# Latent attention's matmuls put in one chain in source order, with the score tiles taken two key tiles at a time

## The chip, the cores and the metric

The kernel runs on one core of a Trainium2 chip. The metric is the device time of one launch in microseconds, as the median of several runs. The engines that matter are TensorE (PE for its matmuls, PEld for its weight loads), VectorE (DVE), ScalarE (ACT) and GpSimd (POOL). Each engine takes its instructions from a queue of its own and in the order of that queue.

## The reference, cut to what matters

The reference is a two-layer network over 1024 latent tokens and 256 context tokens (T = 1280 columns in the kernel, context first), width 1024. Each layer projects its input, mixes tokens in three head groups (gated linear attention, retention, and eight heads of multi-head latent attention), projects out, and runs a gated convolutional feed-forward part. The change touches only the latent attention, which is:

```
s = (einsum('bqhd,bkhd->bhqk', qn, kn) + einsum('bqhr,bkr->bhqk', qr, kr)) * MLA_SCALE
p = softmax(s)
out = einsum('bhqk,bkhe->bqhe', p, v)
```

A latent query sees all 1280 keys. A context query sees the 256 context keys, and is needed in layer 0 alone. Everything is float32.

## The kernel before, in words

The program is one core's instruction stream, traced by a tile framework. The framework knows what each instruction reads and writes. At compile time its scheduler walks through all of them, with its own estimate of their durations, and fixes the order of every engine's queue: of the instructions whose inputs it takes to be ready, the earlier in the source goes first, but one that is not ready is passed by a later one. On the chip the order of each queue is then fixed, and semaphores hold an instruction until what it depends on is done. A manual dependency of the class NoSync adds an edge for the scheduler alone. It adds no semaphore between two instructions of one engine.

In each layer `tile_hybrid_kernel` (L1247) runs the projections, then `weave` (L1233) interleaves two generators: `lin` (L817; linear attention and retention) takes 1.5 steps for each step of `mla` (L826). Their instructions share PE, DVE, ACT and POOL. After them come the output projection and the feed-forward part, whose matmuls are on L323 and L1188.

`mla` handles the heads one after the other. For a head and one tile of 128 keys (`kt`), queries come in two blocks of 512 (`i`). `products` (L938, matmul on L942) makes one score tile of 128 keys by 512 queries with three matmuls that add up in one PSUM bank (high part times high part, and two cross terms with a low part; operands of type float32r). ACT takes the exponential on L1026 into the buffer `held[kt]`, which has room for both query blocks. `values` (L944, matmul on L948) multiplies the exponentials with the values. It issues two plain float32 matmuls, one for each query block, each with 64 columns of weights and 512 moving columns, and they write the lower and upper 64 partitions of bank 6. A float32 matmul is executed as two instructions, so one call of `values` appears as four PE instructions (x4) in the trace.

The source order before: for each key tile, query block 0's three score matmuls, a piece of side work, query block 1's three, a piece of side work, then `values` of the key tile two earlier. The sum of the exponentials is kept by additions on POOL (L1037, key tiles 1 to 6) and DVE (L1035, key tiles 8 and 9; L1043 joins both). The buffers come from a ring of seven (`w2`, L123).

The side work (`beside`, two generator steps after each score tile) prepares the next head: `prod_kq` (L885) makes its keys and queries by matmuls on L903 and L906, which take PSUM banks 0 to 2 at once, with copies by ACT (L912) and DVE (L913). `maxima` (L916) then finds each query's largest score: 24 matmuls (26 in layer 0) on L925, each into one of the banks 0 to 2 in turn, and each followed by a maximum on DVE (L926) that frees the bank. L928, L932 and two DMAs through DRAM bring the negative maxima into row 96 of the next head's queries, which is the 97th row of its score matmuls. Every second head `prod_v` (L854, L858) makes the values of two heads; `prod_qr` (L864) runs twice per layer. `quotient` (L951) ends a head: it copies bank 6, sums the exponentials over keys by matmuls with ones (L959) into one of the banks 0 to 2, takes the reciprocal on DVE (L960) and multiplies on DVE (L963); `tail` runs one step of it. The score tiles rotate through banks 3 to 5.

Of `lin`, the lines that appear below are L739 and L727 (matmuls), L643 and L647 (matmuls of a chunk's output).

Of the kernel before, what the change touches and what calls it, by code (L numbers as in the profile page):

```python
# [9 lines left out]
F32 = mybir.dt.float32  # L10
# [10 lines left out]
CTX = 256  # L21
# [53 lines left out]
class Net:  # L75
# [750 lines left out]
    def mla(self, l, S):  # L826
# [24 lines left out]
        def three():  # L851
            return self.ps[:, base[0]:base[0] + 3, :].rearrange("p a b -> p (a b)")

        def prod_v(p):  # L854
            V[p] = [self.hid([128, 5, 128]) for _ in range(2)]
            ps = three()
            for t_ in range(10):
                nc.tensor.matmul(ps[:, 128 * t_:128 * t_ + 128], S.ckv[:, 128 * t_:128 * t_ + 128], wk[:, 1, 128 * p:128 * p + 128],  # L858
                                 start=True, stop=True)
            for i in range(2):  # L860
                nc.scalar.copy(V[p][i][:].rearrange("p a b -> p (a b)"), ps[:, 640 * i:640 * i + 640])
            yield

        def prod_qr(x):  # L864
            QR[x] = [self.yk(F32R), self.yk(F32R)]
            ps, raw = three(), QR[x][1]
            chunks = [(o, min(512, T - o), ps[:, o - lo:min(512 + o, T) - lo]) for o in range(lo, T, 512)]
            for o, n, t in chunks:
                for kc in range(2):
                    nc.tensor.matmul(t, wr[:, kc, 128 * x:128 * x + 128], S.cq[kc][:, o:o + n], start=(kc == 0), stop=(kc == 1))  # L870
                nc.scalar.copy(raw[:, o:o + n].bitcast(F32), t)
            for o, n, t in chunks:
                r = raw[:, o:o + n].bitcast(F32)
                t2, co, si = self.tt([128, 512]), self.tt([128, 512]), self.tt([128, 512])
                nc.sync.dma_start(co[:, 0:n], a["mcos"][:, o:o + n])
                nc.sync.dma_start(si[:, 0:n], a["msin"][:, o:o + n])
                nc.tensor.matmul(t, self.permm[:], r, start=True, stop=True)
                nc.vector.tensor_tensor(t2[:, 0:n], t, si[:, 0:n], op=ALU.mult)
                nc.vector.tensor_tensor(r, r, co[:, 0:n], op=ALU.mult)
                nc.vector.tensor_tensor(r, r, t2[:, 0:n], op=ALU.add)  # L880
                self.split(QR[x][0][:, o:o + n], raw[:, o:o + n], r)
                del t2, co, si
            yield

        def prod_kq(h):  # L885
            K = Kt[h % 2]
            Q[h] = [self.hs([128, T]) for _ in range(2)]
            rr = slice(32 * (h % 4), 32 * (h % 4) + 32)
            for x in range(2):
                for o in range(lo, T, 512):  # L890
                    c = slice(o, min(o + 512, T))
                    nc.sync.dma_start(Q[h][x][64:96, c].bitcast(F32), QR[h // 4][x][rr, c].bitcast(F32))
            if h < 2:
                for b in range(2):
                    cs = slice(640 * b, 640 * b + 640)
                    self.split(K[0][64:96, cs], K[1][64:96, cs], S.kr[b][64:96, :])
            if h == 1:
                S.kr.clear()
            yield
            ps = three()  # L900
            for o, t, kb in ((CTX, ps[:, 0:512], 1), (CTX + 512, ps[:, 512:1024], 1), (0, ps[:, 1024:1280], 0)):
                n = 512 if kb else CTX
                nc.tensor.matmul(t[0:64, 0:n], wk[:, 0, 64 * h:64 * h + 64], S.ckv[:, o:o + n], start=True, stop=True, skip_group_check=True)  # L903
                if o >= lo:
                    for kc in range(2):
                        nc.tensor.matmul(t[64:128, 0:n], wn[:, kc, 64 * h:64 * h + 64], S.cq[kc][:, o:o + n],  # L906
                                         start=(kc == 0), stop=(kc == 1), skip_group_check=True)
            for o, t, n in ((CTX, ps[:, 0:1024], 1024), (0, ps[:, 1024:1280], CTX)):
                for X, r in ((K, 0), (Q[h], 64)):
                    if r and o < lo:  # L910
                        continue
                    nc.scalar.copy(X[0][0:64, o:o + n], t[r:r + 64])  # L912
                    nc.vector.tensor_tensor(X[1][0:64, o:o + n], t[r:r + 64], X[0][0:64, o:o + n].bitcast(F32), op=ALU.subtract)  # L913
            yield

        def maxima(h):  # L916

            k0, q0 = Kt[h % 2][0], Q[h][0]
            mx, part = self.sm([128, 10]), self.sm([128, 8, 3])
            for qi in range(lo // 128, 10):  # L920
                nk = CTX if qi < 2 else T
                for j, o in enumerate(range(0, nk, 512)):
                    n = min(512, nk - o)
                    t = bank("pre")[:, 0:n]
                    nc.tensor.matmul(t, q0[0:96, 128 * qi:128 * qi + 128], k0[0:96, o:o + n], start=True, stop=True)  # L925
                    nc.vector.tensor_reduce(mx[:, qi:qi + 1] if qi < 2 else part[:, qi - 2, j:j + 1], t, axis=AX.X, op=ALU.max)  # L926
                    yield
            nc.vector.tensor_reduce(mx[:, 2:10], part[:], axis=AX.X, op=ALU.max)  # L928
            yield
            n = 10 - lo // 128  # L930
            t, r = bank("pre"), self.dgt()
            nc.tensor.matmul(t[0:n, 0:128], mx[:, 10 - n:10], self.ident[:], start=True, stop=True)  # L932
            nc.scalar.activation(r[0:n, :], t[0:n, 0:128], AF.Copy, scale=-1.0)
            nc.sync.dma_start(S.mx[h, 10 - n:10, :], r[0:n, :].bitcast(F32))
            nc.sync.dma_start(q0[96:97, lo:T].bitcast(F32), S.mx[h:h + 1].rearrange("h a b -> h (a b)")[:, lo:T])
            yield

        def products(h, kt, c0, t):  # L938

            n = t.shape[-1]  # L940
            for x, (qa, ka, rows) in enumerate(((0, 0, 97), (1, 0, 96), (0, 1, 96))):
                nc.tensor.matmul(t, Kt[h % 2][ka][0:rows, 128 * kt:128 * kt + 128], Q[h][qa][0:rows, c0:c0 + n], start=(x == 0), stop=(x == 2))  # L942

        def values(h, kt, P, n, last):  # L944
            r = 64 * (h % 2)
            op = self.pb("av")
            for i in range(2):
                nc.tensor.matmul(op[64 * i:64 * i + 64, 0:n], V[h // 2][kt // 5][:, kt % 5, r:r + 64], P[:, i], start=(kt == 0), stop=last,  # L948
                                 skip_group_check=True)

        def quotient(h, c0, n, P):  # L951

            r = 64 * (h % 2)
            o, ov, rb = ob[h // 2], self.tt([128, n]), self.tt([128, n])
            nc.scalar.copy(ov[:], self.pb("av")[:, 0:n])
            yield
            t = bank("pre")[:, 0:n]
            for i in range(2):
                nc.tensor.matmul(t[64 * i:64 * i + 64, :], self.ones[:, 0:64], P[:, i], start=True, stop=True, skip_group_check=True)  # L959
            nc.vector.reciprocal(rb[:], t)  # L960
            yield
            for i in range(2):
                nc.vector.tensor_tensor(o[r:r + 64, c0 + n * i:c0 + n * i + n], ov[64 * i:64 * i + 64, :], rb[64 * i:64 * i + 64, :], op=ALU.mult)  # L963
            if h % 2:
                nc.sync.dma_start(S.m[:, 4 + h // 2, c0:c0 + 2 * n], o[:, c0:c0 + 2 * n])
            yield
# [3 lines left out]
                yield from g  # L970

        tails = []

        def tail():
            if tails and next(tails[0], self) is self:
                tails.pop(0)
# [7 lines left out]
        for h in range(8):  # L984
# [11 lines left out]
            def beside(n=2):  # L996
                for _ in range(n):
                    next(side, None)
# [17 lines left out]
                del P  # L1016
                yield
            held = {}
            for kt in range(12):
                if kt < 10:  # L1020
                    held[kt] = self.w2([128, 2, 512], F32)
                for i in range(2):
                    if kt < 10:
                        t = bank("sc")
                        products(h, kt, CTX + 512 * i, t)
                        nc.scalar.activation(held[kt][:, i], t, AF.Exp, scale=MSCALE)  # L1026
                        beside()
                    if i == 0:
                        tail()
                    elif kt >= 2:  # L1030
                        k = kt - 2
                        P = held[k]
                        values(h, k, P, 512, k == 9)
                        if k in (8, 9):
# [3 lines left out]
                        if k not in (0, 7):  # L1038
                            del held[k]
                        del P  # L1040
                    if kt < 10:
                        yield
            nc.vector.tensor_tensor(held[0][:], held[0][:], held[7][:], op=ALU.add)  # L1043
            tails.append(quotient(h, CTX, 512, held[0]))
            tail()
# [431 lines left out]
```

## Time and profile before

| what | value |
|---|---|
| median of 3 runs | 3635.89 us (3632.38 to 3640.07) |
| the profiled execution's own time | 3636.93 us |
| its span, first to last instruction | 3635.2 us |
| PE busy over the span | 3471.4 us (95%) |
| DVE / ACT / POOL busy | 2331.7 / 1410.1 / 561.8 us |
| mean granted clock of TensorE | 0.968 |

A busy PE is a PE with a matmul in flight, not one at its peak. Two stretches hold the woven attention: 365 to 905 us (layer 0) and 2325 to 2768 us (layer 1). In a timeline row the first number is the start, the second the time that the merged row is busy; where the next matmul starts is in the next row.

### The profile page before, as it was taken

What the parts mean: (1) busy time and instruction counts of PE and PEld (TensorE: products, weight loads), DVE (VectorE), ACT (ScalarE), POOL (GpSimd) and SP (SyncE); (2) the same over time, 40 slices, a digit from 0 to 9 for tenths busy, and PEclk for the clock granted to TensorE, in tenths of its full rate; (3) what the DMA queues carried; (4) which work ended last, traced back from release to release, by engine and by line L of the source; (5) the groups of instructions that cost most, each with busy time, mean ns of one, the idle gap of its engine ahead of it and who ended that gap; (6) DMA issues with size and microseconds to landing.
All of it is one profiled execution on the core that took longest, in us unless ns stands there. A gap on an engine that the chain in (4) does not pass through costs nothing. (4 is left out here: it accounts for less than half of the span.)

```text
span 3635.2 us, 50748 instructions
## 1 busy us (share of the span) xinstructions
PE 3471.4 (95%) x20270; PEld 2749.7 (76%) x20270; DVE 2331.7 (64%) x3371; ACT 1410.1 (39%) x2355; POOL 561.8 (15%) x583
## 2 busy tenths in 40 slices
PE   8998999997999999999999999889999999999998
PEld 6995544443999999899999897444446788888897
DVE  4336678777676445675557734878776875577555
ACT  3333333333354332343334443333333554345433
POOL 0001454444011000000000000453441000000001
PEclk9998899998999999999999999899999999999999
DMA  8653011021322333432223444011114222323221
GB/s 293 199 175 112 26 31 46 30 82 63 126 72 99 118 118 130 156 103 78 76 76 115 154 132 138 23 35 38 33 48 155 93 93 93 97 90 116 94 95 51
DMA packets 174702, 354.63 MB, mean 98 GB/s; under 512 B 15648, under 2 KB 92912, under 8 KB 174464
## 3 DMA queue, kind: packets, MB, share of 16 engines
q1 hardware_dynamic: 174464, 351.38, 29.5%
q8 instruction: 159, 2.61, 0.3%
q14 instruction: 79, 0.65, 0.1%
HBM read 310.09 MB, written 36.51 MB: 95 GB/s over the span
## 5 line engine op out<-in xcount | busy, mean ns | idle before, releaser
L323 PE MATMUL ps<-h,w 128*128 128x320 f32 (+5 forms) x9600 | 1681.6, 336 | 27.5 <-ACT h L212 16.4
L323 PEld LDWEIGHTS ps<-h,w 128*128 128x128 f32 x9600 | 1539.6, 190 | 166.3 <-ACT h L212 18.7
L213 DVE TENSOR_TENSOR w<-ws,w 128x1024 fp32r<-128x1024 f32 x360 | 440.2, 1223 | 589.7 <-PE ps L323 289.1
L1188 PE MATMUL ps<-hid,w 128*128 128x256 f32 (+4 forms) x3696 | 576.3, 316 | 1.5 <-ACT hid L212 1.5
L1188 PEld LDWEIGHTS ps<-hid,w 128*128 128x128 f32 x3696 | 538.9, 189 | 35.9 <-issue 7.6
L212 ACT CAST w<-ws 128x1024 fp32r<-128x1024 f32 x360 | 379.1, 1054 | 415.4 <-PE ps L1188 290.9
L1026 ACT ACTIVATE w<-ps 128x512 f32<-128x512 f32 x320 | 188.7, 596 | 338.5 <-PE ps L942 332.4
L942 PE MATMUL ps<-h,h 96*128 96x512 f32 (+3 forms) x1008 | 318.7, 431 | 0.3 <-ACT w L1026 0.2
L942 PEld LDWEIGHTS ps<-h,h 96*128 96x128 f32 (+1 forms) x1008 | 183.3, 199 | 151.8 <-issue 92.2
L926 DVE TENSOR_REDUCE sm<-ps 128x1 f32<-128x512 f32 (+1 forms) x400 | 221.7, 585 | 92.2 <-PE ps L925 90.3
L1037 POOL TENSOR_TENSOR w<-w,w 128x1024 f32<-128x1024 f32 x96 | 238.7, 2487 | 271.1 <-PE ps L948 173.0
L948 PE MATMUL ps<-w,hid 128*64 128x512 f32 (+1 forms) x704 | 276.0, 614 | 0.3 <-ACT w L1005 0.3
L1145 POOL MEMSET u<- 128x1 f32 (+1 forms) x264 | 21.5, 103 | 1613.4 <-DVE t L1156 1486.7
L1155 DVE SCALAR_TENSOR_TENSOR t<-u,vec,t 128x642 f32<-128x642 f32 (+3 forms) x176 | 144.6, 822 | 183.8 <-ACT t L1154 183.6
L1149 ACT COPY u<-ps 128x512 f32<-128x512 f32 (+4 forms) x264 | 118.4, 483 | 316.3 <-PE ps L323 316.3
L1193 DVE SCALAR_TENSOR_TENSOR y<-ps,mod,y 128x320 f32<-128x320 f32 (+5 forms) x376 | 197.1, 558 | 68.5 <-PE ps L1188 68.0
L925 PE MATMUL ps<-h,h 96*128 96x512 f32 (+1 forms) x400 | 156.1, 440 | 34.5 <-DVE sm L926 25.3
L925 PEld LDWEIGHTS ps<-h,h 96*128 96x128 f32 x400 | 77.8, 206 | 126.5 <-DVE sm L926 66.6
L716 POOL TENSOR_TENSOR hid<-hid,hid 128x512 f32<-128x512 f32 x108 | 153.3, 1439 | 83.0 <-ACT hid L696 56.2
L1154 ACT ACTIVATE t<-u,vec 128x642 f32<-128x642 f32 (+3 forms) x176 | 153.7, 873 | 0.4
L1156 DVE SCALAR_TENSOR_TENSOR t<-u,vec,t 128x642 f32<-128x642 f32 (+3 forms) x176 | 144.3, 820 | 11.4
L212 ACT CAST hid<-t 128x642 fp32r<-128x642 f32 (+3 forms) x88 | 59.5, 676 | 204.8 <-DVE t L1160 204.8
(197 smaller groups left out, 3134.4 us busy)
## 6 DMA issues: line engine op xcount, KB each, us to landing
ws<-in_up_dram SPq DMA_DIRECT2D x176, 512.0 KB
ws<-in_down_dram SPq DMA_DIRECT2D x88, 512.0 KB
ws<-in_ada_dram SPq DMA_DIRECT2D x80, 512.0 KB
ws<-in_w_in_dram SPq DMA_DIRECT2D x48, 512.0 KB
ws<-in_w_out_dram SPq DMA_DIRECT2D x32, 512.0 KB
y<-in_ada_dram SPq DMA_DIRECT2D x16, 512.0 KB
ws<-in_w_v_dram SPq DMA_DIRECT2D x16, 512.0 KB
hid<-in_xT_dram SPq DMA_DIRECT2D x16, 320.0 KB
```

What stands on the lines that cost most here:

```text
L212: self.nc.scalar.copy(hi, src)
L213: self.nc.vector.tensor_tensor(lo, src, hi.bitcast(F32), op=ALU.subtract)
L323: nc.tensor.matmul(ps[:, i, 0:n], w_[:, k, :], h[k][:, part, o:o + n], start=(k == 0 and q == 0), stop=(k == 7 and q == 2))
L925: nc.tensor.matmul(t, q0[0:96, 128 * qi:128 * qi + 128], k0[0:96, o:o + n], start=True, stop=True)
L926: nc.vector.tensor_reduce(mx[:, qi:qi + 1] if qi < 2 else part[:, qi - 2, j:j + 1], t, axis=AX.X, op=ALU.max)
L942: nc.tensor.matmul(t, Kt[h % 2][ka][0:rows, 128 * kt:128 * kt + 128], Q[h][qa][0:rows, c0:c0 + n], start=(x == 0), stop=(x == 2))
L948: nc.tensor.matmul(op[64 * i:64 * i + 64, 0:n], V[h // 2][kt // 5][:, kt % 5, r:r + 64], P[:, i], start=(kt == 0), stop=last, skip_group_c ...
L1026: nc.scalar.activation(held[kt][:, i], t, AF.Exp, scale=MSCALE)
L1037: nc.gpsimd.tensor_tensor(held[0][:], held[0][:], P[:], op=ALU.add)
L1154: nc.scalar.activation(v[:, 0:n], u[:, 1:1 + n], AF.Identity, scale=cw(j, 1), bias=self.vec[l][:, V_CB + j:V_CB + j + 1])
L1188: nc.tensor.matmul(pb[i][:, 0:n], w[w_][:, x, ms], p.hh[f0 + x][hp][:, o - 1:o - 1 + n], start=(x == 0 and q == 0), stop=(x == gn - 1 and ...
L1193: nc.vector.scalar_tensor_tensor(t, pb[i][:, o:o + n], self.md(l, 5, m, who), t, op0=ALU.mult, op1=ALU.add)
```

## The change

Every matmul that `mla` issues goes through a new function `pin`, which makes each depend, for the scheduler alone, on the one that `mla` issued before it. So PE's queue holds all of `mla`'s matmuls in the order of the source. `lin`'s matmuls are not pinned and may still be placed between any two of them. And the loop over key tiles takes two at a time: both tiles' four score tiles (twelve matmuls) with their side work, then a step of the tail, then `values` of the two preceding key tiles, one after the other. The number of steps that the generator yields for a head stays 20.

```diff
+        prev = [None]
+
+        def pin(x):
+
+            if prev[0] is not None:
+                self.tc.add_manual_dep(x.ins, prev[0].ins.name, mybir.DependencyInfo(mybir.DependencyClass.NoSync, mybir.DependencyReason.DATA),
+                                       reason="in order")
+            prev[0] = x
+
...
-                nc.tensor.matmul(t, Kt[h % 2][ka][0:rows, 128 * kt:128 * kt + 128], Q[h][qa][0:rows, c0:c0 + n], start=(x == 0), stop=(x == 2))
+                pin(nc.tensor.matmul(t, Kt[h % 2][ka][0:rows, 128 * kt:128 * kt + 128], Q[h][qa][0:rows, c0:c0 + n], start=(x == 0), stop=(x == 2)))
...
-            for kt in range(12):
+            for kt in range(0, 12, 2):
                 if kt < 10:
-                    held[kt] = self.w2([128, 2, 512], F32)
-                for i in range(2):
-                    if kt < 10:
-                        t = bank("sc")
-                        products(h, kt, CTX + 512 * i, t)
-                        nc.scalar.activation(held[kt][:, i], t, AF.Exp, scale=MSCALE)
-                        beside()
-                    if i == 0:
-                        tail()
-                    elif kt >= 2:
-                        k = kt - 2
+                    for k in (kt, kt + 1):
+                        held[k] = self.w2([128, 2, 512], F32)
+                        for i in range(2):
+                            t = bank("sc")
+                            products(h, k, CTX + 512 * i, t)
+                            nc.scalar.activation(held[k][:, i], t, AF.Exp, scale=MSCALE)
+                            beside()
+                            if k == kt or i == 0:
+                                yield
+                tail()
+                if kt >= 2:
+                    for k in (kt - 2, kt - 1):
                         P = held[k]
                         values(h, k, P, 512, k == 9)
...
-                    if kt < 10:
-                        yield
+                if kt < 10:
+                    yield
```

The matmuls of `prod_v`, `prod_qr`, `prod_kq`, `maxima`, `values` and `quotient` are wrapped in `pin` in the same way.

## Rows read from the trace of the kernel before

**Rows 1.** The page's first part: busy time, share, instructions.
```profile
PE 3471.4 (95%) x20270; PEld 2749.7 (76%) x20270; DVE 2331.7 (64%) x3371; ACT 1410.1 (39%) x2355; POOL 561.8 (15%) x583
```

**Rows 2.** Windows: stretch, us, then PE, PEld, DVE, ACT, POOL busy; clock, DMA.
```profile
365.00:905.00 540.00, 491.47 (x2208) 243.66 (x2208) 411.54 (x564) 188.94 (x394) 237.32 (x141) 0.91 0.15 46
2325.00:2768.00 443.00, 411.10 (x1798) 200.54 (x1796) 341.31 (x436) 157.45 (x308) 198.10 (x114) 0.95 0.16 50
...
617.00:628.00 11.00, 8.93 (x48) 5.18 (x49) 10.21 (x13) 3.23 (x9) 8.08 (x6) 0.54 0.18 50
750.00:850.00 100.00, 89.94 (x438) 43.99 (x437) 87.45 (x118) 35.61 (x81) 46.72 (x28) 0.97 0.24 78
850.00:910.00 60.00, 43.20 (x181) 20.74 (x181) 36.65 (x45) 18.07 (x29) 14.03 (x13) 0.84 0.27 86
```

**Rows 3.** Windows of line L948 alone: PE and PEld busy, clock, DMA.
```profile
365.00:905.00 540.00, 146.84 (x384) 30.49 (x384) 0.91 0.15 46
2325.00:2768.00 443.00, 123.77 (x304) 24.17 (x304) 0.95 0.16 50
```

**Rows 4.** PE's timeline in layer 0: start, busy us, line, tiles, shape, count.
```profile
503.25 1.08 PE L948 MATMUL ps<-w,hid 128*64 128x512 f32 x4
504.25 1.66 PE L942 MATMUL ps<-h,h 97*128 97x512 f32 x6
505.84 0.64 PE L948 MATMUL ps<-w,hid 128*64 128x512 f32 x1
...
511.13 1.07 PE L948 MATMUL ps<-w,hid 128*64 128x512 f32 x2
512.13 0.38 PE L925 MATMUL ps<-h,h 96*128 96x256 f32 x1
...
513.45 0.50 PE L942 MATMUL ps<-h,h 97*128 97x512 f32 x1
513.79 0.40 PE L925 MATMUL ps<-h,h 96*128 96x512 f32 x1
514.02 0.62 PE L942 MATMUL ps<-h,h 96*128 96x512 f32 x2
514.48 0.39 PE L925 MATMUL ps<-h,h 96*128 96x512 f32 x1
```

**Rows 5.** DVE's groups in 365 to 905: count, busy, mean ns, idle before, releaser.
```profile
L926 DVE TENSOR_REDUCE sm<-ps 128x1 f32<-128x512 f32 (+1 forms) x182 | 99.8, 578 | 40.3 <-PE ps L925 39.3
L960 DVE RECIPROCAL t<-ps 128x128 f32<-128x128 f32 (+1 forms) x16 | 34.5, 2153 | 5.4 <-PE ps L959 5.3
L963 DVE TENSOR_TENSOR y<-t,t 64x128 f32<-64x128 f32 (+1 forms) x30 | 31.1, 1035 | 0.5
L1035 DVE TENSOR_TENSOR w<-w,w 128x1024 f32<-128x1024 f32 x16 | 25.6, 1597 | 4.3 <-PE ps L948 3.9
L913 DVE TENSOR_TENSOR h<-ps,h 64x256 fp32r<-64x256 f32 (+1 forms) x25 | 19.5, 801 | 5.7 <-ACT h L912 5.5
L1043 DVE TENSOR_TENSOR w<-w,w 128x1024 f32<-128x1024 f32 x8 | 9.7, 1217 | 0.1
```

**Rows 6.** PE's groups in 365 to 905, the same columns.
```profile
L942 PE MATMUL ps<-h,h 97*128 97x512 f32 (+1 forms) x528 | 167.8, 434 | 0.2 <-ACT w L1026 0.2
...
L925 PE MATMUL ps<-h,h 96*128 96x512 f32 (+1 forms) x182 | 68.3, 424 | 12.1 <-DVE sm L926 8.0 <-ACT hid L771 2.9 <-DVE h L913 1.1
...
L906 PE MATMUL ps<-y,ws 128*64 128x512 f32 (+1 forms) x72 | 28.3, 536 | 0.0
L903 PE MATMUL ps<-y,ws 128*64 128x512 f32 (+1 forms) x36 | 17.6, 585 | 0.9 <-ACT hid L861 0.9
```

**Rows 7.** PE's timeline between two heads of layer 0; idle before and releaser in brackets.
```profile
617.52 1.77 PE L858 MATMUL ps<-ws,y 128*128 128x128 f32 x8 [1.67 <-DVE sm L926]
...
620.58 2.07 PE L858 MATMUL ps<-ws,y 128*128 128x128 f32 x8 [0.36 <-ACT dg L933]
623.51 1.97 PE L903 MATMUL ps<-y,ws 128*64 128x512 f32 x2 [0.86 <-ACT hid L861]
```

More of the change, by code (lines that the diff above doesn't have):

```diff
@@ L857, in prod_v @@
             for t_ in range(10):
-                nc.tensor.matmul(ps[:, 128 * t_:128 * t_ + 128], S.ckv[:, 128 * t_:128 * t_ + 128], wk[:, 1, 128 * p:128 * p + 128],
-                                 start=True, stop=True)
+                pin(nc.tensor.matmul(ps[:, 128 * t_:128 * t_ + 128], S.ckv[:, 128 * t_:128 * t_ + 128], wk[:, 1, 128 * p:128 * p + 128],
+                                 start=True, stop=True))
             for i in range(2):
@@ L869, in prod_qr @@
                 for kc in range(2):
-                    nc.tensor.matmul(t, wr[:, kc, 128 * x:128 * x + 128], S.cq[kc][:, o:o + n], start=(kc == 0), stop=(kc == 1))
+                    pin(nc.tensor.matmul(t, wr[:, kc, 128 * x:128 * x + 128], S.cq[kc][:, o:o + n], start=(kc == 0), stop=(kc == 1)))
                 nc.scalar.copy(raw[:, o:o + n].bitcast(F32), t)
@@ L876, in prod_qr @@
                 nc.sync.dma_start(si[:, 0:n], a["msin"][:, o:o + n])
-                nc.tensor.matmul(t, self.permm[:], r, start=True, stop=True)
+                pin(nc.tensor.matmul(t, self.permm[:], r, start=True, stop=True))
                 nc.vector.tensor_tensor(t2[:, 0:n], t, si[:, 0:n], op=ALU.mult)
@@ L902, in prod_kq @@
                 n = 512 if kb else CTX
-                nc.tensor.matmul(t[0:64, 0:n], wk[:, 0, 64 * h:64 * h + 64], S.ckv[:, o:o + n], start=True, stop=True, skip_group_check=True)
+                pin(nc.tensor.matmul(t[0:64, 0:n], wk[:, 0, 64 * h:64 * h + 64], S.ckv[:, o:o + n], start=True, stop=True, skip_group_check=True))
                 if o >= lo:
                     for kc in range(2):
-                        nc.tensor.matmul(t[64:128, 0:n], wn[:, kc, 64 * h:64 * h + 64], S.cq[kc][:, o:o + n],
-                                         start=(kc == 0), stop=(kc == 1), skip_group_check=True)
+                        pin(nc.tensor.matmul(t[64:128, 0:n], wn[:, kc, 64 * h:64 * h + 64], S.cq[kc][:, o:o + n],
+                                         start=(kc == 0), stop=(kc == 1), skip_group_check=True))
             for o, t, n in ((CTX, ps[:, 0:1024], 1024), (0, ps[:, 1024:1280], CTX)):
@@ L924, in maxima @@
                     t = bank("pre")[:, 0:n]
-                    nc.tensor.matmul(t, q0[0:96, 128 * qi:128 * qi + 128], k0[0:96, o:o + n], start=True, stop=True)
+                    pin(nc.tensor.matmul(t, q0[0:96, 128 * qi:128 * qi + 128], k0[0:96, o:o + n], start=True, stop=True))
                     nc.vector.tensor_reduce(mx[:, qi:qi + 1] if qi < 2 else part[:, qi - 2, j:j + 1], t, axis=AX.X, op=ALU.max)
@@ L931, in maxima @@
             t, r = bank("pre"), self.dgt()
-            nc.tensor.matmul(t[0:n, 0:128], mx[:, 10 - n:10], self.ident[:], start=True, stop=True)
+            pin(nc.tensor.matmul(t[0:n, 0:128], mx[:, 10 - n:10], self.ident[:], start=True, stop=True))
             nc.scalar.activation(r[0:n, :], t[0:n, 0:128], AF.Copy, scale=-1.0)
@@ L947, in values @@
             for i in range(2):
-                nc.tensor.matmul(op[64 * i:64 * i + 64, 0:n], V[h // 2][kt // 5][:, kt % 5, r:r + 64], P[:, i], start=(kt == 0), stop=last,
-                                 skip_group_check=True)
+                pin(nc.tensor.matmul(op[64 * i:64 * i + 64, 0:n], V[h // 2][kt // 5][:, kt % 5, r:r + 64], P[:, i], start=(kt == 0), stop=last,
+                                 skip_group_check=True))
         def quotient(h, c0, n, P):
@@ L958, in quotient @@
             for i in range(2):
-                nc.tensor.matmul(t[64 * i:64 * i + 64, :], self.ones[:, 0:64], P[:, i], start=True, stop=True, skip_group_check=True)
+                pin(nc.tensor.matmul(t[64 * i:64 * i + 64, :], self.ones[:, 0:64], P[:, i], start=True, stop=True, skip_group_check=True))
             nc.vector.reciprocal(rb[:], t)
```

## The prediction, made before the changed kernel was run

> **What bounds the kernel now.** I read the page's first part first: PE is busy for 95% of the span and DVE for 64% [rows 1]. Then the windows by stage. The change touches two stretches, 540 us of layer 0 and 443 us of layer 1, 983 us together. In them PE is busy 491 + 411 = 903 us and DVE 412 + 341 = 753 us, at a granted clock of 0.91 and 0.95 [rows 2]. So PE paces the stretches, with DVE not far behind, and there are only 49 + 32 = 81 us without a matmul in flight. A gain must come from PE work that can go, and the next question is whether those 903 us are needed.
>
> For that I read PE's timeline [rows 4]. A row of L948 with x4 is one whole call of `values`, both query blocks: it starts at 503.25 and the next matmul at 504.25, 1.00 us for four instructions. At 511.13 stands a row with x2, half a call, and the next matmul starts at 512.13: again 1.00 us, for half the work. The two query blocks use different halves of the weight columns and run side by side if they follow each other in the queue. If a maximum's matmul (L925) or a score stands between them, each half takes the whole time. So PE is busy with calls that the scheduler has torn apart.
>
> **The change part by part.**
>
> *Halves brought together.* Layer 0's stretch holds 8 heads x 10 key tiles = 80 calls with 512 columns and 16 with 128 for the context; 96 x 4 = 384 instructions, the count in the row. All whole they would be busy 80 x 1.08 = 86.4 us, and the small ones some 16 x 0.4 = 6 us (an estimate: a quarter of the columns of the 1.08 us row, and a tail). The row says 146.84 us [rows 3]. Part of that is the lower clock. A mean of 0.91 means that the work done is 0.91 of that at the full clock: 146.84 x 0.91 = 133.6, less 92.4 is 41 us. Layer 1: 304 instructions are 76 calls; 123.77 x 0.95 = 117.6, less 76 x 1.08 = 82.1, is 35.5 us. Together 77 us at the full clock, so about half of the 156 large calls are torn. After the change both halves are neighbours in the chain, their inputs have been ready for at least four score tiles, and only a matmul of `lin` can be put between. I take all 77 us; the bounds are 0 (all stay torn) and 77.
>
> *Fewer visits.* Six score matmuls from 504.25 to the next value product at 505.84 take 1.59 us. A score or maximum inside a run takes 0.23 us (513.79 to 514.02; two in 514.02 to 514.48), so six cost 1.38 and the two changes of kind 0.21 us; half of it shows at 513.45, where the first score after a value product takes 0.34 us [rows 4]. After the change there are 5 visits to `values` per head, 80 in all. Before there are at most 156 + 77 = 233, if each call and each torn half is a visit of its own; I take 160, since some stand together. That saves 80 x 0.21 = 17 us, between 0 and 32.
>
> PE's saving is thus 94 us at the full clock, about 101 us at the stretches' own clock. PE's demand falls from 903 to some 802 us.
>
> *The chain itself* executes nothing. Its cost is that a matmul of `mla` that must wait now holds all later ones of `mla`; only `lin` can fill. The most frequent waiter is the maximum's matmul: three banks, and each is free only when DVE has reduced it. I work this out for a head of layer 0 [rows 5, 6]. The 26 maxima now belong to the first 13 of its 20 score tiles. DVE's work that falls there, if it holds its place in the source: the maxima 99.8 / 7 = 14.3 us (seven heads are prepared in the stretch), the quotients (34.5 + 31.1) / 8 = 8.2, the split of keys and queries 19.5 / 8 = 2.4, and 13/20 of the rest, (411.5 - 99.8 - 34.5 - 31.1 - 25.6 - 19.5 - 9.7) / 8 = 23.9, so 15.5: 40 us. PE's work there, after the change: 13 x 3 x 0.23 = 9.0 of scores, 16 x 0.23 + 10 x 0.12 = 4.9 of maxima (the short ones half as wide), six calls and three visits 6.6, keys and queries (28.3 + 17.6) / 8 = 5.7, and 13/20 of what is left, (491.5 - 167.8 - 146.8 - 68.3 - 28.3 - 17.6) / 8 = 7.8, so 5.1: 31 us. In this part of a head DVE is thus 9 us over PE, and in the rest (7 score tiles) it is about even: on DVE L1035 and L1043 (25.6 + 9.7) / 8 = 4.4 and 8.4 of the rest; on PE 4.8 of scores, 4.4 of values and 2.7 of the rest. Before the change those 9 us were not paid, as scores and values overtook the maxima, which ran until the end of the head (`prod_v` at 617.52 waits for the last ones [rows 7]). Now they are paid, unless DVE's `lin` work falls back behind the maxima. Bounds over 16 heads: 0 and 146 us.
>
> Which value? DVE's 753 us of work stay. In the two stretches it is 77% busy, in the 100 us from 750 it reaches 87% [rows 2]. With PE's demand at 802 us neither engine can hide the other any more. At 82%, midway between the two rows, the stretches take 753 / 0.82 = 918 us, 65 us less than 983. At 87% they take 865, 118 less, which is more than PE's saving of 101 allows; at 79% 953, 30 less.
>
> *Edits at nothing.* The tail step moves from after the first to after the fourth score tile. Its matmul (L959) waits for L1043; the new order puts four calls of `values`, 4 us, before the head's end, and L1035 twice and L1043 take 1.6 + 1.6 + 1.2 = 4.4 us, so it is covered to within half a microsecond per head. Without that cover it costs up to 4.4 us per head. Two buffers are taken at once: five or six of seven are live, POOL's additions free them within two pairs of key tiles. The exponential is unchanged. No DMA is added or moved, and the queues of SP and POOL get the same instructions.
>
> *The ends of heads.* Before, the last maxima, `prod_v` and `prod_kq` followed each other with nothing between: from 617.52 to 625 PE waits on DVE and ACT again and again [rows 7], and the clock falls to 0.54 [rows 2]. In the chain the maxima are done at score tile 13 to 14 of 20, so this string moves into the head. Against that, `prod_kq` is followed by matmuls that need its copies, with one score tile or none to cover them. I put gain and loss at 8 us of cost, 0.5 us per head, between -30 and +50.
>
> **The sum.** 65 us less from DVE's share, 8 us more: 57 us less. The profiled execution took 3636.9 us, 1 us above the median, so about 3580 us. Its own range, from 79% with the 8 us to PE's full saving less 20: 3555 to 3615.
>
> **A rule that speaks against it.** The granted clock is 0.97 from 750 to 850, where PE is busy 90%, and 0.84 from 850 to 910, where it is 72% [rows 2]: a PE that waits more gets the lower of its two levels, 1.2 against 2.4 GHz, more often. The Trainium skill says the same of short waits (TensorE: Matmul & The Clock Gate, section A second HAM failure mode: psum-queue depth-cycling): small idle stretches between groups of matmuls that cycle through PSUM banks let the clock swing, and throughput falls though single matmuls look normal. Nothing in the sum hangs on that sentence; the rows alone give rival C.
>
> **The rivals.**
>
> A. PE's saving arrives whole, and the waits between heads go too. For it: DVE waits 39 us for the maxima's matmuls in layer 0 [rows 5], so it has slack if they come earlier. Against it: DVE's share would have to pass 85% throughout. Time: 3637 - 101 - 10 = 3526 us.
>
> B. Slower: the maxima wait for DVE, and the chain makes everything wait with them. The place is the first 13 score tiles of a head, the price up to 9 us per head, 146 us in all, against 94: 3637 + 52 = 3689 us. It decides from 5.9 us per head (94 / 16). For it: DVE would have 40 us of work there to PE's 31. Against it: DVE's order is the scheduler's too, and `lin` has no deadline within the head.
>
> C. The clock gives it back. If the stretches ran at 0.84 in place of 0.93, PE would do 0.09 x 900 = 81 us less work in them, and with 60 us of gain the rest is 3637 - 60 + 65 = 3642 us, taking four fifths of the 81. For it: the row at 0.84. Against it: that row is the end of the stage, where work runs out.
>
> D. The change does not do what it says: `lin`'s float32 matmuls are placed between the halves, as they are free to be. Then only visits are saved, less a little waiting: 3637 - 10 = 3627 us. Against it: of the breaks in rows 4 all are maxima and scores, which the chain forbids.
>
> **How the numbers follow.** A measurement tells 0.2%, 7 us, from no change. Forecast 0.52; A 0.16; B 0.14; C 0.08 (faster 0.02, within 7 us 0.03, slower 0.03); D 0.10 (faster 0.05, within 0.05). Faster: 0.52 + 0.16 + 0.02 + 0.05 = 0.75; same: 0.03 + 0.05 = 0.08; slower: 0.14 + 0.03 = 0.17. The range goes from 3525 (A's time; a third of A lies below) to 3648 (C inside, B outside): about 0.2 left out.
>
> **What would show it.** In the changed profile: rows of L948 with x4, x8 and more, few with x2; L948's busy time near 95 us in layer 0 and 85 in layer 1; L942 in runs with L925 only. PE's busy time falls by some 100 us in the two stretches, DVE's stays near 753 us and its share rises above 80%. B would show as long idle times before L925 released by L926, C as a clock under 0.88 in both stretches, D as L727, L739, L643 or L647 between single halves. The prediction is wrong in its main step if L948's busy time does not fall, and in its size if DVE's share stays at 77% while PE's falls.

## The result, and the profile after

| what | before | changed |
|---|---|---|
| median of 4 runs each | 3636.14 us | 3720.82 us (3718.43 to 3726.42) |
| ratio, 95% interval | | 1.0235 (1.0217 to 1.0253) |
| span of the profiled execution | 3635.2 us | 3716.6 us |
| PE / DVE busy over the span | 3471.4 / 2331.7 us | 3420.7 / 2374.6 us |

The change made the kernel 2.35% slower. Forecast were 3580 us and a range from 3525 to 3648. PE is busy for 51 us less, and the kernel takes 85 us more.

The two stretches now run from 365 to 936 us and from 2355 to 2853 us: 571 and 498 us in place of 540 and 443, 86 us more together. All of the loss is in them. The windows of the changed kernel, the same columns as in [rows 2]:

```profile
365.00:936.00 571.00, 454.83 (x2194) 251.87 (x2193) 431.59 (x562) 186.39 (x384) 240.47 (x140) 0.85 0.13 42
2355.00:2853.00 498.00, 408.12 (x1810) 226.01 (x1806) 364.81 (x444) 161.65 (x313) 206.64 (x114) 0.85 0.14 45
```

Four things are to be read against [rows 2]. PE's busy time fell from 903 to 863 us. The time without a matmul rose from 81 to 206 us. The clock fell from 0.91 and 0.95 to 0.85. And DVE, with 796 us of work, is busy for 74% of the stretches, less than the 77% of before: no engine is saturated, PE and DVE wait for each other.

The part of the change that was meant to save did save. The value products' line (L957, before L948), the columns of [rows 3]:

```profile
365.00:936.00 571.00, 103.77 (x376) 29.06 (x376) 0.85 0.13 42
2355.00:2853.00 498.00, 88.51 (x320) 21.93 (x316) 0.85 0.14 45
```

Together the value products are busy for 192 us in place of 271, and that at a lower clock. A run of exactly two instructions of this line is half a call that stands alone (a few are the context's short calls): counted in the traces, there were 147 before and 14 in the changed kernel. PE's timeline of the changed kernel in layer 1 shows the form (columns of [rows 4 and 7]):

```profile
2617.92 1.94 PE L957 MATMUL ps<-w,hid 128*64 128x512 f32 x8
2619.79 0.97 PE L951 MATMUL ps<-h,h 97*128 97x512 f32 x3
2620.59 0.51 PE L934 MATMUL ps<-h,h 96*128 96x256 f32 x2
...
2621.96 0.43 PE L647 MATMUL ps<-t,u 128*64 128x128 f32 x2
2625.34 0.58 PE L934 MATMUL ps<-h,h 96*128 96x256 f32 x1 [2.95 <-DVE sm L935]
```

Two whole calls (x8) take 1.87 us from start to start; torn, as at 511.13 in [rows 4], they would take 4 (an estimate, four halves at 1.00 us). A little later a maximum's matmul (L934, before L925) stands 2.95 us for DVE's reduction (L935), and nothing of the attention may pass it.

A ledger from the windows, estimated as busy time times mean clock: PE's work at the full clock fell from 491 x 0.91 + 411 x 0.95 = 838 to 863 x 0.85 = 734 us, 104 less. At the clock of before (838 / 903 = 0.93) that work would take 790 us, 113 less than 903; the lower clock makes it 863, 73 more; and the waits are 125 more. -113 + 73 + 125 = 85 us, which is the 86 us of the two stretches but for rounding.

PE's waits of the changed kernel, first layer 0, then layer 1 (total us, times, longest):

```profile
PE ps L934 <- DVE sm L935: 32.5, 17, 8.0
PE ps L968 <- DVE h L922: 20.2, 5, 8.2
PE ps L647 <- DVE t L750: 14.5, 3, 7.1
PE ps L941 <- DVE sm L937: 9.8, 3, 6.7
...
PE ps L934 <- DVE sm L935: 25.1, 10, 13.4
PE ps L647 <- DVE t L750: 13.0, 4, 4.7
PE ps L934 <- DVE h L922: 11.6, 5, 2.9
```

Of the 206 us without a matmul some 165 are waits for DVE. The first two kinds of layer 0 are matmuls into the banks 0 to 2: the maxima, and the quotient (L968) behind the copies of the next head's keys (L922). PE's idle time before the maxima is 97.5 us over the span, in place of 34.5. Their group before, and in the changed kernel (count, busy us, mean ns, idle us before, releasers):

```profile
L925 PE MATMUL ps<-h,h 96*128 96x512 f32 (+1 forms) x400 | 156.1, 440 | 34.5 <-DVE sm L926 25.3 <-ACT h L912 4.2 <-ACT hid L771 2.9
L934 PE MATMUL ps<-h,h 96*128 96x512 f32 (+1 forms) x400 | 158.9, 457 | 97.5 <-DVE sm L935 66.0 <-DVE h L922 12.3 <-ACT h L921 9.5
```

The longest of these waits, 13.4 us, shows one way in which DVE gets late. The timeline of PE, DVE and POOL in the changed kernel:

```profile
2688.90 10.63 POOL L1046 TENSOR_TENSOR w<-w,w 128x1024 f32<-128x1024 f32 x4 [41.24 <-PE ps L957]
2689.30 2.54 DVE L338 SCALAR_TENSOR_TENSOR hid<-hid,hid 128x512 f32<-128x512 f32 x1
...
2691.37 0.40 PE L934 MATMUL ps<-h,h 96*128 96x512 f32 x1
...
2691.76 2.82 DVE L972 TENSOR_TENSOR y<-t,t 64x512 f32<-64x512 f32 x1
2694.51 2.82 DVE L339 SCALAR_TENSOR_TENSOR hid<-hid,hid 128x512 f32<-128x512 f32 x1
2697.36 2.72 DVE L972 TENSOR_TENSOR y<-t,t 64x512 f32<-64x512 f32 x1
...
2701.45 0.68 DVE L693 TENSOR_TENSOR hid<-u 128x512 f32<-128x512 f32 x1
2702.05 0.68 DVE L671 TENSOR_TENSOR hid<-hid,hid 128x512 f32<-128x512 f32 x1
...
2704.66 1.01 DVE L935 TENSOR_REDUCE sm<-ps 128x1 f32<-128x256 f32 x2
2705.12 0.58 PE L934 MATMUL ps<-h,h 96*128 96x256 f32 x1 [13.36 <-DVE sm L935]
```

While POOL runs four additions (L1046), the four DVE instructions, all with two inputs in SBUF, take 2.5 to 2.8 us each; once POOL is done, one of the same size (L671) takes 0.68. The reductions that PE waits for stand behind them in DVE's queue. The reductions themselves read PSUM and are not stretched: those of 128x512 take 0.68 us beside an addition and without one (medians of 42 and 202 in this trace). The Trainium skill says this of such pairs (SBUF — State Buffer, section Who interferes with whom): VectorE instructions with two SBUF inputs contend with GpSimd instructions that read SBUF, as they share a read interface. The trace agrees. The price is not a factor but about 2 us for each instruction shown, large or small, nearly the time of one addition (2.4 us at the median). The pair of 64x128 products on L972 takes 0.59 us with POOL idle, and 4.59 us beside additions:

```profile
441.06 0.59 DVE L972 TENSOR_TENSOR y<-t,t 64x128 f32<-64x128 f32 x2
...
752.02 7.26 POOL L1046 TENSOR_TENSOR w<-w,w 128x1024 f32<-128x1024 f32 x3 [1.14 <-PE ps L957]
752.39 4.59 DVE L972 TENSOR_TENSOR y<-t,t 64x128 f32<-64x128 f32 x2
```

### The profile page after: what moved, and what is told of

It is laid out like the page before. It is cut to its first block, busy times and chain, and to the rows that moved or that the text cites. A ratio compares the mean times of both kernels' runs of the same rounds, so it can differ in the third digit from the quotient of the medians.

```text
span 3716.6 us, 50788 instructions
## 1 busy us (share of the span) xinstructions
PE 3420.7 (92%) x20270; PEld 2780.1 (75%) x20270; DVE 2374.6 (64%) x3371; ACT 1412.1 (38%) x2355; POOL 569.3 (15%) x583
## 5 line engine op out<-in xcount | busy, mean ns | idle before, releaser
L951 PE MATMUL ps<-h,h 96*128 96x512 f32 (+3 forms) x1008 | 334.3, 453 | 3.3 <-DMA h<-mx 2.2
L1046 POOL TENSOR_TENSOR w<-w,w 128x1024 f32<-128x1024 f32 x96 | 240.8, 2508 | 416.2 <-PE ps L957 269.6
L951 PEld LDWEIGHTS ps<-h,h 96*128 96x128 f32 (+1 forms) x1008 | 199.1, 215 | 115.3 <-issue 75.3
L935 DVE TENSOR_REDUCE sm<-ps 128x1 f32<-128x512 f32 (+1 forms) x400 | 220.4, 587 | 53.3 <-PE ps L934 51.2
L934 PE MATMUL ps<-h,h 96*128 96x512 f32 (+1 forms) x400 | 158.9, 457 | 97.5 <-DVE sm L935 66.0
L934 PEld LDWEIGHTS ps<-h,h 96*128 96x128 f32 x400 | 89.0, 226 | 150.0 <-DVE sm L935 88.1
L957 PE MATMUL ps<-w,hid 128*64 128x512 f32 (+1 forms) x704 | 194.2, 642 | 0.0
```

The lines of the kernel that those rows point to most:

```text
L934: pin(nc.tensor.matmul(t, q0[0:96, 128 * qi:128 * qi + 128], k0[0:96, o:o + n], start=True, stop=True))
L951: pin(nc.tensor.matmul(t, Kt[h % 2][ka][0:rows, 128 * kt:128 * kt + 128], Q[h][qa][0:rows, c0:c0 + n], start=(x == 0), stop=(x == 2)))
L957: pin(nc.tensor.matmul(op[64 * i:64 * i + 64, 0:n], V[h // 2][kt // 5][:, kt % 5, r:r + 64], P[:, i], start=(kt == 0), stop=last, skip_gro ...
L1046: nc.gpsimd.tensor_tensor(held[0][:], held[0][:], P[:], op=ALU.add)
```

## The experiments

Each run was timed beside the kernel before on the same chip; before's medians there were 3632 to 3637 us. Theory 1 was that the chain does the harm, because a matmul that waits for DVE holds all of the attention; theory 2 that the grouping by two key tiles does.

**The chain alone, and the grouping alone.** The first takes the loop of before with every `pin`, the second the new loop without one.

```diff
-            for kt in range(0, 12, 2):
+            for kt in range(12):
...
```

```diff
-                pin(nc.tensor.matmul(t, Kt[h % 2][ka][0:rows, 128 * kt:128 * kt + 128], Q[h][qa][0:rows, c0:c0 + n], start=(x == 0), stop=(x == 2)))
+                nc.tensor.matmul(t, Kt[h % 2][ka][0:rows, 128 * kt:128 * kt + 128], Q[h][qa][0:rows, c0:c0 + n], start=(x == 0), stop=(x == 2))
...
```

> The loop over key tiles as before (one tile at a time), and every latent-attention matmul chained in source order. Theory 1 (in the chain a maximum's matmul that waits for VectorE holds all of the attention's matmuls behind it): most of the 85 us loss is there, 3690 to 3740 us, with idle time of TensorE before the maxima's matmuls near 100 us as in the changed kernel (97.5), against 34.5 before. Theory 2 (taking two key tiles at a time does the harm: bursts of four score tiles on three banks, the later tail step): 3640 us or less, since the torn value products are whole.

Measured: 3693.5 us, ratio 1.0170 (1.0147 to 1.0194). The time is in theory 1's range. PE's idle time before the maxima is 61.8 us, not near 100; before the quotient's matmuls it is 44.0 us, where the changed kernel has 22.4 and before had 5.5.

> Two key tiles at a time, and no chain. Theory 1: not slower than before by more than 0.5%, 3600 to 3650 us; fewer torn value products than before, so their busy time is between 194 and 276 us, and idle time before the maxima's matmuls stays near 35 us. Theory 2: slower by over 1%, 3680 us or more.

Measured: 3607.4 us, ratio 0.9933 (0.9910 to 0.9956). Its windows, and then PE's group of the maxima over the span:

```profile
365.00:888.00 523.00, 466.99 (x2208) 241.61 (x2208) 412.43 (x564) 186.70 (x393) 237.00 (x141) 0.92 0.15 46
2305.00:2735.00 430.00, 400.30 (x1805) 205.78 (x1804) 330.82 (x438) 157.37 (x310) 201.47 (x117) 0.94 0.16 50
```

```profile
L925 PE MATMUL ps<-h,h 96*128 96x512 f32 (+1 forms) x400 | 159.8, 450 | 32.1 <-DVE sm L926 27.3 <-ACT hid L771 2.9 <-ACT h L912 0.9
```

The chain alone makes the kernel slower, as theory 1 said, and grouping alone does no harm, so theory 2 falls. Grouping alone gains 0.7%: value products are busy 238 us over the span in place of 276, the clock stays, and PE waits before the maxima as little as before. The two don't add, though: grouping gains some 26 us without the chain and costs some 27 with it (3693.5 to 3720.8). No run tests why.

**Which members of the chain.** In the next runs some matmuls of the changed kernel lose `pin`. Of the lines below, the first is a maximum's, the second the quotient's, the third one of the makers'; the run with the maxima free takes the first (and the small transposing matmul that ends them), the one with the quotient free the second, the one with the makers free all of the third kind, the one with scores, maxima and values chained the second and third, and the one with scores and values alone chained all three.

```diff
-                    pin(nc.tensor.matmul(t, q0[0:96, 128 * qi:128 * qi + 128], k0[0:96, o:o + n], start=True, stop=True))
+                    nc.tensor.matmul(t, q0[0:96, 128 * qi:128 * qi + 128], k0[0:96, o:o + n], start=True, stop=True)
...
-                pin(nc.tensor.matmul(t[64 * i:64 * i + 64, :], self.ones[:, 0:64], P[:, i], start=True, stop=True, skip_group_check=True))
+                nc.tensor.matmul(t[64 * i:64 * i + 64, :], self.ones[:, 0:64], P[:, i], start=True, stop=True, skip_group_check=True)
...
-                pin(nc.tensor.matmul(t[0:64, 0:n], wk[:, 0, 64 * h:64 * h + 64], S.ckv[:, o:o + n], start=True, stop=True, skip_group_check=True))
+                nc.tensor.matmul(t[0:64, 0:n], wk[:, 0, 64 * h:64 * h + 64], S.ckv[:, o:o + n], start=True, stop=True, skip_group_check=True)
```

> The changed kernel with the maxima's matmuls (and the small transposing matmul that ends them) left out of the chain. Theory 1: scores and values may pass a waiting maximum again, so at least half of the loss goes: 3610 to 3680 us; some value products are torn again, by maxima. Theory 2, or a loss that comes from the order of the other matmuls: it stays at 3700 us or more.

Measured: 3691.1 us (1.0161; 1.0141 to 1.0182). Less than half of the loss goes, 30 of 85 us: neither theory's range, a miss.

> Two key tiles at a time; only scores and value products are chained, while maxima, quotients and the makers of keys, queries and values are free. If the harm is a waiter of another kind inside the chain (maxima waiting for VectorE, the quotient's and the key makers' matmuls waiting for banks): close to the version without a chain, 3595 to 3630 us. If scores and values in a row are themselves the harm: 3670 us or more, near the 3691 us of the version that frees the maxima alone.

Measured: 3603.9 us (0.9920; 0.9903 to 0.9936). Scores and values in a row are harmless: with grouping this is as fast as grouping without a chain (0.9933), within the intervals.

> Two key tiles at a time; scores, maxima (and the small matmul that ends them) and value products chained, while quotients and the makers of keys, queries and values are free. With maxima free and these chained it was 3691 us, with both free 3604 us. Theory M (a waiting maximum is the harm): 3680 us or more. Theory Q (the quotient and the makers, which wait for the banks of the maxima, are the harm): 3650 us or less. If each brings its part: about 3634 us (3604 + 30, the 30 us that freeing the maxima gave).

Measured: 3697.9 us (1.0172; 1.0146 to 1.0199), theory M's case: maxima in the chain are enough. But the run with the maxima free had shown that the quotient and the makers are enough too.

> The changed kernel with the quotient's matmuls alone out of the chain. TensorE waited 20 us before them in layer 0 of the changed kernel, up to 8.2 us at a time. If the quotient is the main part of the 87 us that the quotient and the makers bring: 3660 us or less. If the makers are: 3700 us or more.

Measured: 3723.4 us (1.0240; 1.0219 to 1.0260): with all else chained, freeing the quotient alone gives nothing.

> The changed kernel with the matmuls that make keys, queries and values alone out of the chain. They wait in the trace of the changed kernel only 8 us themselves, but the maxima behind them wait for their copies. If they are the main part of the 87 us: 3660 us or less; if the quotient is: 3700 us or more.

Measured: 3685.5 us (1.0135; 1.0110 to 1.0160), between its two cases.

So the parts don't add. Maxima in the chain beside scores and values cost 94 us, makers and quotient 87, all of them 117. The question was then whether one member is enough. Scores and values keep `pin`, and so does this line:

```diff
                 pin(nc.tensor.matmul(t[64 * i:64 * i + 64, :], self.ones[:, 0:64], P[:, i], start=True, stop=True, skip_group_check=True))
```

> Two key tiles at a time; scores, value products and the quotient's matmuls chained; maxima and makers free. If any matmul into the three banks that VectorE empties carries its lateness into the chain: 3640 us or more. If only the numerous ones do (26 maxima, 9 matmuls of keys and queries a head): 3600 to 3620 us, like the version with scores and values alone (3604).

Measured: 3693.7 us (1.0163; 1.0147 to 1.0179). The quotient's matmuls, once per head and four instructions, are enough: 90 us more than without them. PE's group of the maxima, first with scores, values and quotient chained, then with scores and values alone:

```profile
L934 PE MATMUL ps<-h,h 96*128 96x512 f32 (+1 forms) x400 | 167.0, 471 | 68.3 <-DVE sm L935 43.9 <-ACT h L921 8.3 <-DVE h L922 7.0
```

```profile
L934 PE MATMUL ps<-h,h 96*128 96x512 f32 (+1 forms) x400 | 158.2, 443 | 32.4 <-DVE sm L935 27.7 <-ACT hid L771 2.9 <-ACT h L921 0.8
```

The code suggests how one reaches all: banks 0 to 2 are handed out in turn in the order of the source. A quotient that is pinned among the scores needs its bank from the maxima and the key makers that had it earlier in the source, so these must all be done before any later score may be issued, whether they are pinned or not. I counted in the traces after how many of a head's 20 score tiles the matmul stands that ends the next head's maxima (L932, L941), for the 14 heads that prepare another: after 18.7 on average before the change (14 to 20), after 14 or 15 in every head of the changed kernel, after 16.4 with the quotient chained, and with scores and values alone chained at the end of the head in 10 of 14. The maxima used to trail, and their waits fell where other matmuls were ready to go. No run gave the quotient a bank of its own, so that the banks carry the order is argued from the code and these counts, and not tested by itself.

> One key tile at a time, as before, with scores and value products chained and all else free. If the 32 us gained by the version with two key tiles and this chain come from the grouping: 3625 to 3645 us, no change from before. If they come from the chain of scores and values: 3610 us or less.

Measured: 3640.5 us (1.0021; 1.0008 to 1.0033). With the loop of before (`for kt in range(12)`) this chain gains nothing, it costs 0.2%: the gain is the grouping's.

**When the side work comes.**

```diff
-                            beside()
+                            beside(1 + i)
```

> The changed kernel with one and two steps of side work after the score tiles in turn, in place of two after each: the maxima of the next head take up about 18 of the 20 score tiles and not 13. Theory 1 with crowding (VectorE has 40 us of work beside TensorE's 31 in the first 13 tiles): the waits before the maxima's matmuls fall by a third or more and the time is 3650 to 3695 us. Without crowding as the cause (VectorE paces the whole head, or the wait is of single long VectorE instructions): 3705 us or more.

Measured: 3692.6 us (1.0166; 1.0142 to 1.0190). The time just falls in the first case, but the waits before the maxima do not: PE's idle time there is 109.2 us, where the changed kernel has 97.5. So crowding in the first 13 score tiles is not what makes PE wait for the maxima; they end after 19 or 20 tiles here and still hold the chain. Where the 28 us came from was not tested (over the span PE is busy for 12 us less and idle for 16 us less).

> Scores and values chained and all else free, and the side work spread as one and two steps in turn. Spreading gave 28 us in the fully chained kernel; if it gives a part of that here, 3585 to 3600 us, the fastest so far. If the free maxima already find their places, it stays at 3600 to 3610 us.

Measured: 3617.7 us (0.9947; 0.9926 to 0.9967): some 10 to 14 us slower than without spreading, neither case. PE's idle time before the maxima is 61.8 us in place of 32.4; why was not tested.

**What makes VectorE late.** In the first run each reduction covers `t[:, 0:128]`; in the others POOL's addition is

```diff
-                            nc.gpsimd.tensor_tensor(held[0][:], held[0][:], P[:], op=ALU.add)
+                            nc.gpsimd.tensor_tensor(held[0][:, 0, 0:64], held[0][:, 0, 0:64], P[:, 0, 0:64], op=ALU.add)
```

> The changed kernel with VectorE's reduction of each maximum's tile over 128 of its columns only (0.2 to 0.25 us in place of 0.59, some 140 us less VectorE work in all), and exponentials at 0.002 of their scale; both leave part of the computation out. Theory 1 (VectorE's lateness holds the chain): at least 60 us less than the changed kernel, 3660 us or below. If the chain hurts by other waits (quotient, banks, the linear part): 3690 us or more.

Measured: 3636.0 us (1.0013; 1.0001 to 1.0024), 85 us less than the changed kernel, as theory 1 wanted. A reduction takes 0.29 us, and DVE is busy for 132 us less over the span. It is not proof that the chain is the whole reason: PE's idle time before the maxima falls only from 97.5 to 75.9 us, and the kernel before was not run with the same cut.

> The changed kernel with each of GpSimd's additions of exponentials (key tiles 1 to 6) cut from 1024 to 64 columns; so that the sums stay finite the exponentials use 0.002 of their scale. Both leave part of the computation out. Theory 1a: the chain hurts because VectorE's instructions on SBUF operands are stretched (0.68 to 2.8 us in the trace) while these additions run, so the maxima come late and hold the chain. Then TensorE's waits for VectorE before the maxima fall by half and the time is 3640 us or less, with little left of the 85 us between changed and before when before has the same cut. Theory 1b (VectorE's order and amount of work alone): the time falls by what before falls too, and the gap between the two stays over 60 us.

Measured: 3568.4 us (0.9821; 0.9802 to 0.9841). PE's waits for the reductions before the maxima fall by half, from 66.0 to 29.4 us:

```profile
L934 PE MATMUL ps<-h,h 96*128 96x512 f32 (+1 forms) x400 | 158.4, 459 | 59.6 <-DVE sm L935 29.4 <-DVE h L922 12.3 <-ACT h L921 7.9
```

> The kernel before with the same cut of GpSimd's additions and the same scale, as the control for the run above. Theory 1a: a fall of 10 to 40 us (to 3595 to 3625 us), less than in the changed kernel, because the maxima's lateness is passed by scores and values here. Theory 1b: the same fall in both.

Measured: 3545.6 us (0.9757; 0.9740 to 0.9773).

> Two key tiles at a time, scores and value products chained, all else free, and GpSimd's additions cut to 64 of 1024 columns with the exponentials at 0.002 of their scale (parts of the computation left out). Before falls by 90 us with this cut, the changed kernel by 152. If the additions' extra harm of 62 us in the changed kernel needs the full chain: a fall of about 90 us here too, to 3505 to 3530 us. If grouping the values makes it: a fall of over 120 us, to 3485 us or less.

Measured: 3509.4 us (0.9660; 0.9643 to 0.9678).

The changed kernel falls by 152 us, before by 90 (expected were 10 to 40) and the grouping with scores and values alone chained by 95. The gap between the changed kernel and before falls from 85 to 23 us: theory 1a for the most part, though before gains more than it said. So the additions do 60 us more harm with the chain than without; the chain's cost against the same kernel with scores and values alone chained is 117 us with full additions and 59 us with small ones. Half of it goes with the additions, half stays. That the additions act by stretching DVE, and not by POOL being late itself, is read from the traces: PE waits for POOL only 13 us in the stretches of the changed kernel, never for an addition, and DVE is busy for 132 us less when they are small. DVE's instructions, shortest, median and longest, in the changed kernel and then with small additions:

```profile
L972 DVE TENSOR_TENSOR y<-t,t x48: 273/686/2821, 380.0 to 2846.6; 64x512 f32<-64x512 f32 x32, 64x128 f32<-64x128 f32 x16
L339 DVE SCALAR_TENSOR_TENSOR hid<-hid,hid x18: 683/1411/2817, 417.1 to 2818.9; 128x512 f32<-128x512 f32 x18
```

```profile
L972 DVE TENSOR_TENSOR y<-t,t x48: 273/685/1435, 381.4 to 2703.4; 64x512 f32<-64x512 f32 x32, 64x128 f32<-64x128 f32 x16
L339 DVE SCALAR_TENSOR_TENSOR hid<-hid,hid x18: 675/685/1782, 409.8 to 2678.0; 128x512 f32<-128x512 f32 x18
```

And before's stretches with small additions, at a clock of 0.96 and 1.00, with 652 us of DVE work in place of 753:

```profile
365.00:848.00 483.00, 464.40 (x2208) 233.22 (x2208) 355.01 (x565) 187.54 (x395) 132.47 (x141) 0.96 0.16 51
2264.00:2675.00 411.00, 398.31 (x1814) 197.81 (x1812) 296.73 (x441) 158.63 (x310) 102.66 (x114) 1.00 0.17 53
```

## Why the prediction was wrong

*Halves brought together, fewer visits*: right in sum. 94 us at the full clock were forecast, the ledger has 104. L957's busy time of 104 and 89 us is near what was said (95 and 85), at a lower clock. By the ledger's estimate the value products alone fell from 251 to 163 us, 88 where 77 were put; and 77 torn calls mean 154 halves alone, where 147 are counted. The visits were sized too low: unbroken runs of value products fell from 240 to 93 (the context's included), where 160 and 80 were taken. What a visit is worth was not measured by itself.

*The chain itself*: the step that failed. Its bounds were 0 and 146 us and contained the 125 us by which the waits grew; the value was then taken from another quantity, DVE's share, and came out as a gain of 65 us. I put that at 82% because PE's demand would no longer hide DVE. But a share of 87% had been reached in a queue order in which matmuls that wait stood late and others before them. The chain removes that order, and DVE's share fell to 74%. With the share left out, the step's own 9 us per head (rival B, 3689 us, chance 0.14) was the better figure: the waits grew by 125 us, 8 us per head. That the two are so close is partly luck. Over the span the idle time before the maxima grew by 63 us (34.5 to 97.5), half of the 125; the rest stands before others, such as the quotient (5.5 to 22.4) and `lin`'s L647 (6.0 to 27.5). Nor did spreading the maxima shorten the waits before them, and the quotient alone, chained with scores and values, cost 90 us. So the place that counts is every bank that DVE must empty, not the first 13 score tiles.

*DVE's work as a constant 753 us*: wrong as a price, 796 us in the changed kernel, and missing as a mechanism. [Rows 5] held the sign: L963's mean is 1035 ns over two shapes, and its longest instance in the trace took 2831 ns. What stretches DVE is not in DVE's own groups but in POOL's.

*The ends of heads*: the maxima did move to tile 14, as said, and `prod_v`'s waits at the end of a head (7.5 us in both stretches) went. But the quotient now waits for the key copies (20.2 us in layer 0), and a maker's matmul (L912) once for 7.8 us: some 16 us of cost in all, where 8 were put.

*Rival C*: the clock fell to 0.85, and the ledger prices that at 73 us, an estimate. The forecast's sum had no term for it. I had B and C as separate cases with 0.14 and 0.08. They come together: the lower of TensorE's two levels (1.2 against 2.4 GHz) was granted more in the kernels that waited more. That the clock would have stayed up without the waits is shown only by the versions without them (0.92 and 0.94 when grouped without a chain); it was not tested by itself.

*Rival D*: not what happened; 14 halves stand alone after the change, where it wanted most of them to.

## What to carry to other kernels

Chain for order only what is ready early and whose buffer a fast engine frees. If a chain contains one instruction whose buffer rotates with those of a slow engine, the users of that rotation that stand earlier in the source are in it too, as far as the counts here show. When an edit takes away overtaking, price the waits of the queue as it will stand, and don't carry over an engine's busy share from a queue that could overtake. Here the grouping without the chain (3607 us), or with scores and values alone chained (3604 us), is what to keep; the two are equal within the noise.

## What the runs showed of the hardware that was not expected

- The value products of two query blocks, on different halves of the weight columns, cost 1.00 us together as neighbours and 1.00 us each when one other matmul stands between them [rows 4]; in the changed kernel two calls in a row take 1.87 us.
- Cutting GpSimd's 96 additions of 128x1024 to 64 columns took 90 us of 3636 off the kernel before, though POOL is busy for only 15% of the span. VectorE's instructions with two SBUF inputs take about 2 us longer beside an addition (2.8 us for 0.68, 2.3 for 0.29), and with the small additions TensorE's time without a matmul in the stretches falls from 81 to 31 us.
- Much the same matmuls of TensorE ran at a clock of 0.85 with 206 us of waits in the stretches, of 0.91 and 0.95 with 81 us.
